# The reciprocal root of each norm in a two-layer decoder trunk: its six short steps on GpSimd's queue instead of VectorE's

## The chip, the core and the metric

The kernel runs on one core of one Trainium2 chip. The core has five engines with a queue of their own each: TensorE (PE in the profile, with PEld for its weight loads), VectorE (DVE), ScalarE (ACT), GpSimd (POOL) and SyncE (SP, which here only issues DMAs). Each engine takes its instructions strictly in the order in which they stand in its queue and waits for semaphores of the others. The metric is the time of one execution on the device in microseconds (us); the number given for a kernel is the median of several runs.

## What is computed

The reference is a decoder trunk of two layers over 256 tokens of width 1024, in float32. Cut to what matters here:

```python
def _rms(x):
    y = xf * lax.rsqrt(jnp.mean(xf * xf, axis=-1, keepdims=True) + EPS)

for l in range(DEPTH):                       # DEPTH = 2
    mod = (silu(c) @ w_ada[l] + b_ada[l]).reshape(B, N_SUB, 3, D_MODEL)
    norm_mod(h, j) = _rms(h) * g_norm[l, j] * (1.0 + scale_j) + shift_j
    x = x + 0.5 * gate(0) * _swiglu(norm_mod(x, 0), w_ffn_up[l, 0], w_ffn_down[l, 0])
    x = x + gate(1) * _mixer(norm_mod(x, 1), ...)
    x = x + 0.5 * gate(2) * _swiglu(norm_mod(x, 2), w_ffn_up[l, 1], w_ffn_down[l, 1])
```

So six norms stand between the sub-layers, and each needs one reciprocal root per token. The mixer has three token mixers (a gated linear recurrence and two kinds of causal attention) between one input and one output projection.

## The kernel before

The 256 tokens are two tiles of 128 partitions, called t = 0 and t = 1 here. A sub-layer ends for a tile with the last products of its down (or output) projection (`dn`, `wo`), after which the next sub-layer's norm of this tile can start; the other tile's products run on TensorE meanwhile.

Every weight arrives as a float32 block `raw` of 128x1024 over SyncE's queue. ScalarE casts it to a high part `H` (L246) and VectorE subtracts to get the low part `L` (L247); these two long instructions, 320 of each, fill most of both engines' queues. Each product is three matmuls (H by high part, L by high part, H by low part of the activations `hTh`, `hTl`). VectorE also makes the modulation (`raw` times `cb`, L292 and L317), where `cb` is silu(c).

One norm of a tile goes through these steps:

1. `residual` (L444, L445 on VectorE): x gets its update, in two halves.
2. `norm_sq` (L396 on ScalarE): the sum of squares of each half into `ss`; L399 adds the halves to `v`.
3. `rsqrt` (L359, then L363 and L364 twice): a first guess of 1/sqrt(v) from the bits of v, and two Newton steps. The result is `ny`. L399 and these five are the six short steps, each on 128x1 elements and each needing the one before.
4. `norm_xn` (L407 on ScalarE): `xn` = x times `ny`, two halves.
5. `norm_out`: TensorE transposes `xn` into `tp` (L418, eight 128x128 pieces in two buffers), ScalarE (L426) and VectorE (L428) make `hf` from it, and L431 to L434 split that into `hTh` and `hTl`, which the next projection (`pj` in the mixer, `up` in the feed-forward part) reads.

The buffers of `tp` are shared with the transposes `tg` (L532) and `tx` (L637) of other work: two in all.

The two norms of the input at the start have no L399 and take their sum of squares on VectorE (L936): 2 chains of five steps, and 10 chains of six later (there is no norm behind the last sub-layer).

The order of the instructions in each queue isn't the order of the code: the framework schedules the program with an estimate of each instruction's duration and writes each queue down in the order that it found. So a change of one engine's work can move rows on all.

Of the kernel before, what the change touches and what calls it, by code (L numbers as in the profile page):

```python
# [12 lines left out]
I32 = mybir.dt.int32  # L13
AF = mybir.ActivationFunctionType
ALU = mybir.AluOpType
# [79 lines left out]
def trunk_kernel(ctx: ExitStack, tc: tile.TileContext, x, c, wst, ada, par, cst, row, wg, out):  # L95
    nc = tc.nc
# [16 lines left out]
    def W2(shape, dt=F32, name="w2"):  # L113
        return w2.tile(shape, dt, tag="w2", name=name)

    def SM(shape, dt=F32, name="sm"):
        return sm.tile(shape, dt, tag="sm", name=name)
# [10 lines left out]
    V, A, T, S = nc.vector, nc.scalar, nc.tensor, nc.sync  # L128
# [224 lines left out]
            ada_step(1)  # L353


    def rsqrt(v, n, name):
        y = SM([128, n], name=name + "y")
        a = SM([128, n], name=name + "a")
        V.tensor_scalar(out=y.bitcast(I32), in0=v.bitcast(I32), scalar1=-0.5, scalar2=float(0x5F1FFFF9),  # L359
                        op0=ALU.mult, op1=ALU.add)  # L360
        for c in (-2.38924456, -3.0 / NEWTON ** 2):
            if n == 1:
                V.tensor_scalar(out=a, in0=y, scalar1=v, scalar2=y, op0=ALU.mult, op1=ALU.mult)  # L363
                V.tensor_scalar(out=y, in0=a, scalar1=c, scalar2=y, op0=ALU.add, op1=ALU.mult)  # L364
            else:
                V.tensor_tensor(out=a, in0=y, in1=y, op=ALU.mult)
                V.tensor_tensor(out=a, in0=a, in1=v, op=ALU.mult)
                V.scalar_tensor_tensor(out=y, in0=a, scalar=c, in1=y, op0=ALU.add, op1=ALU.mult)
        return y


# [12 lines left out]
    xn_t, r_t = {}, {}  # L384

    def norm_in(t):
        norm_sq(t, 2)
        norm_xn(t)

    def norm_sq(t, parts=1):  # L390
        n = D // parts
        ss = SM([128, parts], name="ss")
        for i in range(parts):
            q = slice(i * n, (i + 1) * n + i // (parts - 1) if parts > 1 else D + 1)
            junk = W2([128, D + 1], BF16, name="junk")
            A.activation(junk[:, q], xe[t][:, q], AF.Square, scale=1.0 / 32, accum_out=ss[:, i:i + 1])  # L396
        if parts == 2:
            v = SM([128, 1], name="v")
            V.tensor_tensor(out=v, in0=ss[:, 0:1], in1=ss[:, 1:2], op=ALU.add)  # L399
        else:  # L400
            v = ss
        r_t[t] = rsqrt(v, 1, "n")

    def norm_xn(t):
        xn_t[t] = W4([128, D], name="xn")
        for q in (slice(0, D // 2), slice(D // 2, D)):
            A.activation(xn_t[t][:, q], xt[t][:, q], AF.Copy, scale=r_t[t])  # L407
# [65 lines left out]
    def ffn(l, s, after, pre={}):  # L473
# [66 lines left out]
        def down(j, t):  # L540
            if j == 0:
                dn[t] = [PD([128, 512], name="dn") for _ in range(2)]
            w = [unit(("dn", l, s, j, i)) for i in range(2)]

            order = [(i, n) for i in range(2) for n in range(2)]
            for i, n in sorted(order, key=lambda p: p[1]) if j == NCH - 1 else order:
                q = slice(n * 512, (n + 1) * 512)
                mm3(dn[t][n], *gT[j, i, t], w[i][0][:, q], w[i][1][:, q],
                    j == 0 and i == 0, j == NCH - 1 and i == 1)
            if j == NCH - 1:  # L550
                if after is None:
                    residual(l, j3, t, dn[t], lambda t, q: S.dma_start(out=out[t * 128:(t + 1) * 128, q], in_=xt[t][:, q]))
                    return
                residual(l, j3, t, dn[t])
                norm_sq(t, 2)
                if t == 1:
                    norm_xn(1)
                    pending.append(lambda: after[1](1))
# [373 lines left out]
    for t in range(NT):  # L932
        ss = SM([128, 1], name="ss")
        junk = W2([128, D + 1], BF16, name="junk")
        x1 = xe[t][:, 0:D + 1]
        V.scalar_tensor_tensor(out=junk, in0=x1, scalar=1.0 / D, in1=x1, op0=ALU.mult, op1=ALU.mult, accum_out=ss)  # L936
        r_t[t] = rsqrt(ss, 1, "n")
        norm_xn(t)
    xnT = [W4([128, NT, 4, 128], name="xnT") for _ in range(2)]
    for g in range(2):  # L940
# [7 lines left out]
    for k in range(KT):  # L948
        for v in range(2):
# [3 lines left out]
                        scalar2=S_t[0, 0][:, k:k + 1], op0=ALU.mult, op1=ALU.add)  # L953
# [117 lines left out]
```

## Time and profile before

| | |
|---|---|
| median of 3 runs | 1011.37 us (1008.23 to 1013.19) |
| the profiled execution | 1010.85 us, of which the span from first to last instruction is 1009.0 us |
| TensorE busy | 982.2 us (97%) |
| VectorE busy | 761.4 us (75%), 1224 instructions |
| ScalarE busy | 532.9 us (53%) |
| GpSimd busy | 6.9 us, 16 instructions (12 are DMA issues) |

Rows of the trace give, for a timeline, the start in us, the length in us, the engine, the line of the kernel, the operation, what is written and read, and in brackets how long the engine sat idle before and what ended that. An arrow reads "written from", a number behind x counts merged instructions.

### The profile page before, as it was taken

Reading aid. Unit: us, or ns where it says so; the run is one execution under the profiler, and the core shown is the slowest. Engines: PE = TensorE matmul, PEld = TensorE weight load, DVE = VectorE, ACT = ScalarE, POOL = GpSimd, SP = SyncE. Lnnn points to the kernel's source line nnn. Section 1 sums busy time; section 2 is a strip of 40 time slices with the busy share of each in tenths; the row PEclk is TensorE's granted clock in tenths of the full one; section 3 lists DMA queues with packets and bytes.
Section 4 is the critical chain, followed back from the end, with each engine's and each line's share of the span. In section 5 each row is a group of like instructions: output and inputs, shape, how many; then the busy total and the mean of one; then the engine's idle time right before and its main releaser. Section 6 shows DMA issues by size and latency. Waiting matters only on the chain.

```text
span 1009.0 us, 15828 instructions
## 1 busy us (share of the span) xinstructions
PE 982.2 (97%) x6054; PEld 857.9 (85%) x6054; DVE 761.4 (75%) x1224; ACT 532.9 (53%) x854; POOL 6.9 (1%) x16
## 2 busy tenths in 40 slices
PE   6999999989999999999999999999999999999998
PEld 4999999867867799999878999997788778999996
DVE  8988888788996988888589888765778588636352
ACT  5373435558775534355465344455678655535340
POOL 0000000000000000000000000000000000000000
PEclk9999999999999999999999999999999999999999
DMA  8999999677382999999449999854542349655511
GB/s 320 352 336 341 350 330 342 237 259 268 127 279 96 318 370 331 343 327 329 171 165 339 361 346 335 310 177 157 189 167 84 105 155 343 241 180 192 185 64 42
DMA packets 69966, 251.26 MB, mean 249 GB/s; under 512 B 8066, under 2 KB 8706, under 8 KB 69891
## 3 DMA queue, kind: packets, MB, share of 16 engines
q1 hardware_dynamic: 68834, 247.09, 69.3%
q0 software_dynamic: 1056, 3.17, 1.0%
q8 instruction: 47, 0.77, 0.3%
q14 instruction: 29, 0.23, 0.1%
HBM read 249.16 MB, written 1.07 MB: 248 GB/s over the span
## 4 chain that ended last, share of the span: by engine, by line
PE 86%; DVE 7%; ACT 5%; issue 1%; DMA 1%; ACTq 0%; DVEq 0%; SPq 0%
PE up L470 38%; PE dn L258 8%; PE dn L260 8%; PE dn L259 8%; PE up L271 6%; PE pj L271 5%; PE up L273 3%; PE pj L273 2%; DVE L L247 2%; PE wo L258 1%; PE wo L259 1%; PE wo L260 1%; ACT hf L426 1%; ACT H L246 1%; DVE raw L292 1%
## 5 line engine op out<-in xcount | busy, mean ns | idle before, releaser
L247 DVE TENSOR_TENSOR L<-raw,H 128x1024 fp32r<-128x1024 f32 x320 | 381.5, 1220 | 79.1 <-ACT H L246 78.0
L246 ACT CAST H<-raw 128x1024 fp32r<-128x1024 f32 x320 | 327.9, 1051 | 114.1 <-DMA raw<-in_wst 61.3
L470 PE MATMUL up<-hTh,H 128*128 128x256 f32 x1088 | 209.9, 280 | 2.4 <-ACT H L246 1.9
L470 PE MATMUL up<-hTl,H 128*128 128x256 f32 x1088 | 210.0, 281 | 0.0
L470 PE MATMUL up<-hTh,L 128*128 128x256 f32 x1088 | 209.3, 280 | 0.0
L470 PEld LDWEIGHTS up<-hTh,H 128*128 128x128 f32 x1088 | 167.5, 188 | 8.8 <-ACT H L246 2.3
L470 PEld LDWEIGHTS up<-hTl,H 128*128 128x128 f32 x1088 | 163.8, 188 | 0.3 <-DVE hTl L955 0.3
L470 PEld LDWEIGHTS up<-hTh,L 128*128 128x128 f32 x1088 | 163.9, 189 | 0.0
L462 ACT ACTIVATE sg<-up 128x256 f32<-128x256 f32 x88 | 33.8, 384 | 209.5 <-PE up L470 168.1
L258 PE MATMUL dn<-H,gh 128*128 128x512 f32 x352 | 140.4, 399 | 1.3 <-ACT gh L535 1.1
L260 PE MATMUL dn<-H,gl 128*128 128x512 f32 x352 | 139.7, 397 | 0.0
L259 PE MATMUL dn<-L,gh 128*128 128x512 f32 x352 | 139.0, 395 | 0.0
L292 DVE SCALAR_TENSOR_TENSOR raw<-raw,cb 128x1024 f32<-128x1024 f32 x96 | 114.9, 1219 | 1.8 <-DMA raw<-in_ada 1.4
L260 PEld LDWEIGHTS dn<-H,gl 128*128 128x128 f32 x352 | 66.0, 188 | 16.0 <-DVE gl L536 0.9
L258 PEld LDWEIGHTS dn<-H,gh 128*128 128x128 f32 x352 | 66.2, 188 | 14.9 <-ACT gh L535 3.2
L519 DVE TENSOR_TENSOR sg<-sg,up 128x256 f32<-128x256 f32 x68 | 28.5, 419 | 65.6 <-ACT sg L462 65.1
L259 PEld LDWEIGHTS dn<-L,gh 128*128 128x128 f32 x352 | 66.2, 188 | 12.5
L271 PE MATMUL up<-H,hTh 128*128 128x512 f32 x160 | 64.8, 405 | 0.7 <-DVE hTh L431 0.6
L271 PE MATMUL up<-L,hTh 128*128 128x512 f32 x160 | 63.9, 400 | 0.0
L273 PE MATMUL up<-H,hTl 128*128 128x512 f32 x160 | 57.5, 396 | 0.0
L317 DVE SCALAR_TENSOR_TENSOR raw<-raw,cb 128x1024 f32<-128x1024 f32 x48 | 56.8, 1217 | 0.7 <-DMA raw<-in_ada 0.7
L271 PE MATMUL pj<-H,hTh 128*128 128x512 f32 x128 | 52.5, 410 | 1.2 <-DVE hTh L431 1.2
(229 smaller groups left out, 1051.5 us busy)
## 6 DMA issues: line engine op xcount, KB each, us to landing
raw<-in_wst SPq DMA_DIRECT2D x320, 512.0 KB, 5.2
raw<-in_ada SPq DMA_DIRECT2D x144, 512.0 KB, 5.3
gate<-row POOLq DMA_DIRECT2D x6, 512.0 KB, 6.9
x<-in_x SPq DMA_DIRECT2D x2, 512.0 KB, 4.3
wgt<-in_wg SPq DMA_DIRECT2D x2, 512.0 KB, 6.6
out_x<-x SPq DMA_DIRECT2D x4, 256.0 KB, 2.0
once<-in_cst SPq DMA_DIRECT2D x1, 192.0 KB, 5.4
p_sb<-in_par SPq DMA_DIRECT2D x1, 168.0 KB, 5.2
```

What stands on the lines that cost most here:

```text
L246: A.copy(h, raw)
L247: V.tensor_tensor(out=lo, in0=raw, in1=h.bitcast(F32), op=ALU.subtract)
L258: T.matmul(o, lhsT=xh, rhs=wh, start=first, stop=False)
L259: T.matmul(o, lhsT=xh, rhs=wl, start=False, stop=False)
L260: return T.matmul(o, lhsT=xl, rhs=wh, start=False, stop=last)
L271: T.matmul(o, lhsT=hh[:, k, :], rhs=part, start=k == 0 and i == 0, stop=False)
L273: mul = T.matmul(o, lhsT=hl[:, k, :], rhs=w(k)[0], start=False, stop=k == KT - 1)
L292: V.scalar_tensor_tensor(out=raw, in0=raw, scalar=1.0, in1=cb, op0=ALU.mult, op1=ALU.mult, accum_out=st[:, v, k:k + 1])
L317: V.scalar_tensor_tensor(out=raw, in0=raw, scalar=1.0, in1=cb, op0=ALU.mult, op1=ALU.mult, accum_out=col[:, k:k + 1])
L462: used.append(A.activation(*a, **k))
L470: return T.matmul(o[:, v], lhsT=w[:, q:q + 128], rhs=(hTh, hTl)[h][:, :, k, :], start=opens, stop=True, skip_group_check=True)
L519: V.tensor_tensor(out=sg, in0=sg, in1=o[:, 1], op=ALU.mult)
```

## The change

`rsqrt` and the addition of the two halves in `norm_sq` name GpSimd instead of VectorE. The arithmetic is the same. 70 short instructions (12 chains: 2 of five and 10 of six) leave VectorE's queue and come into GpSimd's.

```diff
-    def rsqrt(v, n, name):
-        y = SM([128, n], name=name + "y")
-        a = SM([128, n], name=name + "a")
-        V.tensor_scalar(out=y.bitcast(I32), in0=v.bitcast(I32), scalar1=-0.5, scalar2=float(0x5F1FFFF9),
+    def rsqrt(v, name):
+
+        G = nc.gpsimd
+        y = SM([128, 1], name=name + "y")
+        a = SM([128, 1], name=name + "a")
+        G.tensor_scalar(out=y.bitcast(I32), in0=v.bitcast(I32), scalar1=-0.5, scalar2=float(0x5F1FFFF9),
                         op0=ALU.mult, op1=ALU.add)
         for c in (-2.38924456, -3.0 / NEWTON ** 2):
-            if n == 1:
-                V.tensor_scalar(out=a, in0=y, scalar1=v, scalar2=y, op0=ALU.mult, op1=ALU.mult)
-                V.tensor_scalar(out=y, in0=a, scalar1=c, scalar2=y, op0=ALU.add, op1=ALU.mult)
...
+            G.tensor_scalar(out=a, in0=y, scalar1=v, scalar2=y, op0=ALU.mult, op1=ALU.mult)
+            G.tensor_scalar(out=y, in0=a, scalar1=c, scalar2=y, op0=ALU.add, op1=ALU.mult)
         return y
...
-            V.tensor_tensor(out=v, in0=ss[:, 0:1], in1=ss[:, 1:2], op=ALU.add)
+            nc.gpsimd.tensor_tensor(out=v, in0=ss[:, 0:1], in1=ss[:, 1:2], op=ALU.add)
```

Line numbers behind `rsqrt` are smaller by three in the changed kernel (L404 is what L407 was, L415 what L418 was). In GpSimd's queue each step waits on a semaphore for the one before; ahead of the first step stands one new instruction, a reload of the engine's library that waits for nothing. The DMA issues of `row` and `gate`, which were the queue's only work, keep their places between the chains, and none of them stands between the steps of a chain.

The schedule moves with it. The place shown first is the norm of tile 1 between the first layer's mixer and its second feed-forward part. VectorE's queue there, before:

```order
L445 TENSOR_TENSOR x_89<-x_89,tmp 128x512 x2
L247 TENSOR_TENSOR L<-raw,H 128x1024
L399 TENSOR_TENSOR v<-ss 128x1
L247 TENSOR_TENSOR L<-raw,H 128x1024
L359 TENSOR_SCALAR ny<-v 128x1
L495 TENSOR_TENSOR sg<-sg,up 128x256
L363 TENSOR_SCALAR na<-ny,v 128x1
L247 TENSOR_TENSOR L<-raw,H 128x1024
L364 TENSOR_SCALAR ny<-na,ny 128x1
L247 TENSOR_TENSOR L<-raw,H 128x1024
L363 TENSOR_SCALAR na<-ny,v 128x1
L247 TENSOR_TENSOR L<-raw,H 128x1024
```

And now:

```order
L442 TENSOR_TENSOR x_89<-x_89,tmp 128x512 x2
L247 TENSOR_TENSOR L<-raw,H 128x1024 x4
L492 TENSOR_TENSOR sg<-sg,up 128x256
L247 TENSOR_TENSOR L<-raw,H 128x1024
L425 TENSOR_SCALAR hf<-tp,G_2701,S_2702 128x128 x3
```

The short steps are gone from between the long ones, and four L247 follow each other. ScalarE's queue at the same place, before:

```order
L396 ACTIVATE junk,ss<-x_89 128x513
L246 CAST H<-raw 128x1024
L462 ACTIVATE sg<-up 128x256
L246 CAST H<-raw 128x1024
L407 ACTIVATE xn<-x_89,ny 128x512 x2
L462 ACTIVATE sg<-up 128x256
L426 ACTIVATE hf<-tp,S_2702,G_2701 128x128 x4
```

And now:

```order
L393 ACTIVATE junk,ss<-x_89 128x513
L246 CAST H<-raw 128x1024
L404 ACTIVATE xn<-x_89,ny 128x512 x2
L459 ACTIVATE sg<-up 128x256
L246 CAST H<-raw 128x1024
L423 ACTIVATE hf<-tp,S_2702,G_2701 128x128 x4
```

`xn` now stands ahead of an `sg` and a cast that stood ahead of it. TensorE's queue at the same place, with the tiles' numbers, from the last matmuls of the row `up` of tile 0 on, before:

```order
L273 MATMUL up_3522<-H_3585,hTl_138 128x512
L418 MATMUL tp_3556<-c_sb_94,xn_3467 128x128 x4
L418 MATMUL tp_3568<-c_sb_94,xn_3467 128x128 x4
L532 MATMUL tg_3598<-c_sb_94,sg_3519 128x128 x2
L258 MATMUL dn_3640<-H_3644,gh_3601 128x512
L271 MATMUL up_3605<-H_3473,hTh_137 128x512
```

And now:

```order
L415 MATMUL tp_3556<-c_sb_94,xn_3467 128x128 x4
L415 MATMUL tp_3568<-c_sb_94,xn_3467 128x128 x4
L271 MATMUL up_3522<-H_3549,hTh_137 128x512
L271 MATMUL up_3522<-L_3550,hTh_137 128x512
L273 MATMUL up_3522<-H_3549,hTl_138 128x512
L271 MATMUL up_3522<-H_3585,hTh_137 128x512
L271 MATMUL up_3522<-L_3586,hTh_137 128x512
L273 MATMUL up_3522<-H_3585,hTl_138 128x512
L271 MATMUL up_3522<-H_3585,hTh_137 128x512
L271 MATMUL up_3522<-L_3586,hTh_137 128x512
L273 MATMUL up_3522<-H_3585,hTl_138 128x512
L529 MATMUL tg_3598<-c_sb_94,sg_3519 128x128 x2
```

The eight transposes stand nine matmuls earlier: behind 39 of the 48 matmuls of this row of `up`, not behind all. The other norms of tile 1 move alike: behind 39 instead of 48 in both mixers' input and in the second layer's second feed-forward part (in the second layer's mixer input it was 44), behind 33 instead of 47 in front of the second layer. For tile 0 the transposes move by seven matmuls behind the first feed-forward part of layer 0, and by none or one elsewhere.

The second place is the start of ScalarE's queue, before:

```order
L407 ACT_TABLE_LOAD
L407 ACTIVATE xn<-x_88,ny 128x512
L152 ACTIVATE le<-le 128x8
L154 ACT_TABLE_LOAD
L182 ACTIVATE cb<-pc 128x512 x2
L407 ACTIVATE xn<-x_88,ny 128x512
L407 ACTIVATE xn<-x_89,ny 128x512 x2
```

And now:

```order
L152 ACT_TABLE_LOAD
L152 ACTIVATE le<-le 128x8
L154 ACT_TABLE_LOAD
L182 ACTIVATE cb<-pc 128x512
L404 ACTIVATE xn<-x_88,ny 128x512
L182 ACTIVATE cb<-pc 128x512
L404 ACTIVATE xn<-x_88,ny 128x512
L404 ACTIVATE xn<-x_89,ny 128x512 x2
```

The first half of `xn` stood ahead of everything; now it stands between the two halves of `cb`.

## Rows read from the trace of the kernel before

**Rows 1.** The page: busy times by engine, and one of its costliest groups.

```profile
PE 982.2 (97%) x6054; PEld 857.9 (85%) x6054; DVE 761.4 (75%) x1224; ACT 532.9 (53%) x854; POOL 6.9 (1%) x16
...
L246 ACT CAST H<-raw 128x1024 fp32r<-128x1024 f32 x320 | 327.9, 1051 | 114.1 <-DMA raw<-in_wst 61.3
```

**Rows 2.** Stretches around the norms: busy time by engine, granted clock, DMA share, GB/s.

```profile
190.00:230.00 40.00, 35.91 (x157) 27.54 (x156) 31.93 (x64) 23.39 (x40) 1.09 (x2) 0.96 0.64 221
300.00:345.00 45.00, 43.12 (x195) 33.92 (x193) 36.33 (x71) 26.85 (x49) 0.00 (x0) 1.00 0.55 186
345.00:495.00 150.00, 150.00 (x1028) 138.53 (x1027) 120.62 (x168) 67.48 (x91) 1.09 (x2) 1.00 0.93 331
495.00:540.00 45.00, 43.90 (x201) 34.99 (x200) 35.55 (x67) 24.45 (x44) 0.00 (x0) 1.00 0.47 158
690.00:725.00 35.00, 33.52 (x154) 26.44 (x154) 26.60 (x48) 24.69 (x41) 0.00 (x0) 1.00 0.46 150
790.00:835.00 45.00, 43.12 (x194) 33.76 (x189) 32.11 (x62) 24.18 (x45) 0.00 (x0) 0.96 0.44 147
```

**Rows 3.** Waits: engine, line, releaser: us in total, times, longest.

```profile
ACT xn L407 <- DVE ny L364: 25.7, 8, 5.9
PE tg L532 <- ACT hf L426: 3.1, 3, 1.0
PE tx L637 <- ACT lxt L634: 2.4, 2, 1.7
```

**Rows 4.** Timeline, VectorE: first and last steps of tile 1's norm behind layer 0's mixer.

```profile
326.92 0.16 DVE L399 TENSOR_TENSOR v<-ss 128x1 f32<-128x1 f32 x1
327.00 1.22 DVE L247 TENSOR_TENSOR L<-raw,H 128x1024 fp32r<-128x1024 f32 x1
...
332.42 0.21 DVE L364 TENSOR_SCALAR ny<-na,ny 128x1 f32<-128x1 f32 x1
```

**Rows 5.** Timelines of ScalarE and TensorE at the same place.

```profile
326.69 0.20 ACT L396 ACTIVATION_READ_ACCUMULATOR junk<-x 128x1 f32 x1
...
332.66 1.34 ACT L407 ACTIVATE xn<-x,ny 128x512 f32<-128x512 f32 x2 [3.56 <-DVE ny L364]
334.19 1.50 ACT L426 ACTIVATE hf<-tp,S,G 128x128 f32<-128x128 f32 x4
...
321.87 0.50 PE L271 MATMUL up<-H,hTh 128*128 128x512 f32 x1 [0.28 <-DVE hTh L431]
...
333.44 1.27 PE L418 MATMUL tp<-c_sb,xn 128*128 128x128 f32 x8
335.75 0.44 PE L532 MATMUL tg<-c_sb,sg 128*128 128x128 f32 x2 [1.04 <-ACT hf L426]
336.65 0.50 PE L258 MATMUL dn<-H,gh 128*128 128x512 f32 x1 [0.46 <-ACT gh L535]
```

**Rows 6.** Timeline, VectorE: first and last of six steps with nothing between them.

```profile
504.61 0.15 DVE L399 TENSOR_TENSOR v<-ss 128x1 f32<-128x1 f32 x1
...
505.86 0.21 DVE L364 TENSOR_SCALAR ny<-na,ny 128x1 f32<-128x1 f32 x1
```

**Rows 7.** Timeline, GpSimd: one of its four memsets and one of its DMA issues.

```profile
0.28 0.10 POOL L1060 MEMSET const-float32-1.0<- 128x1 f32 x1
...
549.02 0.54 POOL L324 DMA_DIRECT2D row<-gt  x1 [184.12 <-DVE gt L322]
```

**Rows 8.** Stretches of 4 us behind two of TensorE's pauses, columns as in rows 2.

```profile
224.00:228.00 4.00, 4.00 (x15) 3.24 (x14) 2.00 (x5) 1.64 (x2) 0.54 (x1) 0.68 0.51 169
828.00:832.00 4.00, 4.00 (x14) 3.15 (x13) 4.00 (x8) 1.38 (x2) 0.00 (x0) 0.66 0.63 209
```

**Rows 9.** Timeline of the start.

```profile
5.67 0.15 DVE L359 TENSOR_SCALAR ny<-ss 128x1 int32<-128x1 int32 x1
...
9.10 1.09 ACT L182 ACTIVATE cb<-pc 128x512 f32<-128x512 f32 x2
...
10.62 1.22 DVE L292 SCALAR_TENSOR_TENSOR raw<-raw,cb 128x1024 f32<-128x1024 f32 x1
```

More of the change, by code (lines that the diff above doesn't have):

```diff
@@ L353, in ada_until @@
             ada_step(1)
-    def rsqrt(v, n, name):
-        y = SM([128, n], name=name + "y")
-        a = SM([128, n], name=name + "a")
-        V.tensor_scalar(out=y.bitcast(I32), in0=v.bitcast(I32), scalar1=-0.5, scalar2=float(0x5F1FFFF9),
+    def rsqrt(v, name):
[3 more added lines that the diff above has]
+        G.tensor_scalar(out=y.bitcast(I32), in0=v.bitcast(I32), scalar1=-0.5, scalar2=float(0x5F1FFFF9),
                         op0=ALU.mult, op1=ALU.add)
         for c in (-2.38924456, -3.0 / NEWTON ** 2):
-            if n == 1:
-                V.tensor_scalar(out=a, in0=y, scalar1=v, scalar2=y, op0=ALU.mult, op1=ALU.mult)
-                V.tensor_scalar(out=y, in0=a, scalar1=c, scalar2=y, op0=ALU.add, op1=ALU.mult)
[L365 to L368, printed above, removed]
+            G.tensor_scalar(out=a, in0=y, scalar1=v, scalar2=y, op0=ALU.mult, op1=ALU.mult)
+            G.tensor_scalar(out=y, in0=a, scalar1=c, scalar2=y, op0=ALU.add, op1=ALU.mult)
         return y
@@ L398, in norm_sq @@
             v = SM([128, 1], name="v")
-            V.tensor_tensor(out=v, in0=ss[:, 0:1], in1=ss[:, 1:2], op=ALU.add)
+            nc.gpsimd.tensor_tensor(out=v, in0=ss[:, 0:1], in1=ss[:, 1:2], op=ALU.add)
         else:
             v = ss
-        r_t[t] = rsqrt(v, 1, "n")
+        r_t[t] = rsqrt(v, "n")
     def norm_xn(t):
@@ L936, in trunk_kernel @@
         V.scalar_tensor_tensor(out=junk, in0=x1, scalar=1.0 / D, in1=x1, op0=ALU.mult, op1=ALU.mult, accum_out=ss)
-        r_t[t] = rsqrt(ss, 1, "n")
+        r_t[t] = rsqrt(ss, "n")
         norm_xn(t)
```

## The prediction

> **What bounds the kernel now.** I read the page's busy times first: TensorE is busy 97% of the span, VectorE 75% and GpSimd 1% [rows 1]. So what a change can win is TensorE's idle time, and I looked for it by stretches. Between the norms there is none: 345 to 495 us is 150.00 busy of 150 [rows 2]. Around the norms there is: 4.09, 1.88, 1.10, 1.48 and 1.88 us in the five stretches, together 10.4 us [rows 2]. The waits say who holds things up: ScalarE's `xn` waits 25.7 us in 8 waits for the last short step on VectorE, and TensorE's `tg` waits for `hf`, three steps behind `xn` [rows 3].
>
> The timeline shows why the root is late. Behind layer 0's mixer the sum of squares of tile 1 is ready at 326.89 (326.69 + 0.20) [rows 5]; the last step ends at 332.63 (332.42 + 0.21) [rows 4]. The chain takes C = 5.7 us, because each step waits behind a long instruction such as the 1.22 us of L247 [rows 4]. With nothing between them six steps take 1.46 us (504.61 to 506.07) [rows 6]. TensorE meanwhile comes to `tg` and waits 1.04 us for the buffer that `hf` must free, then 0.46 us for `gh` [rows 5].
>
> **The change, part by part.** It removes the steps from VectorE. I count nothing for VectorE's own time: it isn't the bound, and its work behind 326 us is casts for weights that TensorE needs later.
>
> It puts the steps on GpSimd. No row shows such a step there. The nearest from below is GpSimd's memset, 0.10 us, which makes 0.6 us for six; the nearest from above is its DMA issue, 0.54 us, 3.2 us for six [rows 7]. VectorE's own six give 0.24 each (1.46 / 6) [rows 6]. A dependent step with scalars from memory is nearer to the issue than to a memset, and I take 0.45, so 2.7 us. To this I add 0.9 us for meeting VectorE (three quarters of one 1.22 us instruction [rows 4]), which gives C = 3.6 us. The bound from above is a step that each time waits out a long instruction: 6 x 1.22 + 2.7 = 10 us.
>
> What C may be is set by TensorE's new order. At the place of rows 5 the row of `up` starts at 321.87 and its 48 matmuls end with the transposes' start at 333.44, 0.241 us each. Behind 39 of them the transposes are due at 331.27. A half of `xn` takes some 0.67 us (1.34 for two), so the root must be there by 330.6, C at most 3.7. `hf` must be done when TensorE comes to `tg`, at 334.7 as before (333.44 + 1.27; the same work in another order). In the old order `hf` ends 3.03 us after `xn` starts (332.66 to 334.19 + 1.50), with an `sg` between; the new order adds a cast of 1.05 us [rows 1], so 4.1 us, which again asks for 330.6 [rows 5]. So with C = 3.6 the two waits of 1.5 us go, and with C = 5.4 they are back in another place.
>
> The five stretches one by one at C = 3.6. Of the 10.4 us of idle time some stays: `tx` follows `pj` directly in the new order too and waits for a copy of its last result, some 0.7 us in each layer (2.4 us in two waits, the longest 1.7 [rows 3]), and 0.28 us before `up` of tile 0 behind each mixer, where the transposes don't move [rows 5]. That leaves 10.4 - 1.4 - 0.6 = 8.4 us. At the layer boundary the transposes move by 14 matmuls, not 9, so that C may be only some 3.0 us there: 0.6 back. Small overshoots at the other places: 0.4.
>
> Behind two of the pauses the granted clock falls between its two levels, to 0.68 and 0.66 over 4 us [rows 8], which is (0.32 + 0.34) x 4 = 2.6 us of TensorE's time. At a pause of about the same size, behind layer 0's mixer, the stretch 300 to 345 shows 1.00 [rows 2]. I count half, 1.3 us.
>
> The start: `xn` of tile 0 now stands between the halves of `cb`, and VectorE's first long instruction on `cb` starts at 10.62 [rows 9]. The sum of squares is there at 5.67; with C = 2.7 + 0.9, less one step, a half of `xn` and half of the 1.09 us of `cb`, it would be 5.67 + 3.2 + 0.7 + 0.5 = 10.1. I book 0.5 us of loss for the library's reload ahead of it, whose length no row shows. More is hidden by nothing: every us over 10.62 delays the modulation that TensorE's first projection waits for.
>
> The Trainium skill (GPSIMD Engine Reference, Instruction dispatch) gives about 6 us for the first call to freshly loaded code on this engine, with no instruction visible. If that runs from the program's start, it would end at about 7 us and cost an estimated 1.5 us more, so the sum would be 1.5 us smaller by it; no row here shows it.
>
> Sum: 8.4 + 1.3 - 0.6 - 0.4 - 0.5 = 8.2 us. The profiled execution took 1010.85 us, so 1002.6; the median of the runs is 0.5 above it, and I forecast **1003 us**.
>
> Beyond 3.6 us every us of C costs on seven chains (five of tile 1, two of tile 0 behind feed-forward parts), about 7 us per us of C, as TensorE stands in order behind its earlier transposes. The gain is used up at C = 3.6 + 8.2 / 7 = 4.8 us.
>
> **The rivals.**
>
> *The two engines hold each other up.* Before, VectorE's queue was what paced the steps. If a step of GpSimd can't start while a long VectorE instruction with two inputs in SBUF runs, the pace stays: the queue shows four L247 in a row at this place, and VectorE is busy nearly throughout. v waits from 326.9 to 328.2, then 0.45, then 1.22, and so on until the fourth L247 is done; then VectorE waits for `sg`, which now stands behind `xn`, and the last two steps run free. 1.3 + 3 x 1.2 + 3 x 0.45 ends near 333, C about 5.5 to 6 here, 2.7 behind the mixers for tile 0, where VectorE has nothing to do, and about 5 on the mean. Against the forecast that is 7 x 1.4 = 9.8 us: 1013 us, in a range from 1009 to 1017. For it: VectorE's 36.33 of 45 us [rows 2]. Against: nothing in the trace shows GpSimd beside VectorE at all; its issue of 0.54 us was no longer than the others.
>
> The Trainium skill (SBUF — State Buffer, Who interferes with whom) states this rule: an instruction of VectorE with two SBUF inputs contends with one of GpSimd that reads SBUF, and whichever starts first keeps the shared port pair to its end. By it the time would be that of this rival. No run shown so far bears it out or against it.
>
> *The steps themselves are slow.* At 1 us each, with nothing in their way, C is 6 everywhere: 8.2 - 2.4 x 7 = -8.6, so 1020 us, slower. It decides from 0.8 us for a step on. For it: apart from memsets the only job of this engine in the trace takes 0.54 us [rows 7]. Against: its memset took 0.10.
>
> *The reload is long.* If the engine is ready at 15 us, the start comes 8 us later and eats the gain: 1011 us.
>
> *The gain is taken elsewhere.* The earlier `xn` pushes casts of weights and `sg` back on ScalarE, and TensorE waits for those: 1007 us. Against it: DMA and ScalarE have room (a DMA share of 0.44 to 0.64 and 23.39 of 40 to 26.85 of 45 us [rows 2]).
>
> **How the numbers follow.** The forecast 0.42; the engines holding each other up 0.25; gain taken elsewhere 0.16; slow steps 0.10; reload 0.07. The range for 8 in 10 goes from 998 (everything won, with the full clock part) to 1016. The forecast's own range is 999 to 1006. A measurement of this kernel tells 0.5%, 5 us, from no change (its own runs lie 5 us apart). Faster by over 0.5%: the forecast's 0.42 and 0.05 of the others, 0.47. Slower: slow steps 0.10 and 0.09 of the lock and the reload, 0.19. Within: 0.34.
>
> **What would show it.** GpSimd's six steps with a start-to-start near 0.45 us, and chains of 3 to 4 us from the end of `junk` to `xn`. `xn`'s waits down from 25.7 us to some 10. TensorE's idle time in the five stretches down from 10.4 to about 3, `tg`'s wait for `hf` gone, and the granted clock 1.00 behind 224 us and 828 us. The forecast is wrong if steps start only where VectorE's long instructions end, if a step takes 0.8 us or more alone, or if VectorE's first instruction on `cb` starts later than 11 us.

## The result

The changed kernel takes 1019.61 us (median of 6 runs, 1015.95 to 1022.91) against 1011.42 us: a ratio of 1.0082, with a 95% interval from 1.0065 to 1.0099. The change made the kernel slower by 0.8%, where 1003 us had been forecast. The profiled run took 1017.62 us, its span 1015.8 us.

The busy times by stretch, as in [rows 2], a little longer where the work now ends later:

```profile
190.00:232.00 42.00, 37.11 (x160) 28.24 (x159) 30.82 (x49) 24.61 (x41) 12.33 (x14) 0.96 0.56 196
300.00:347.00 47.00, 44.73 (x204) 35.00 (x204) 33.72 (x62) 25.78 (x47) 6.36 (x12) 1.00 0.48 160
...
495.00:542.00 47.00, 44.70 (x198) 35.81 (x197) 31.42 (x53) 22.84 (x42) 6.77 (x12) 0.96 0.45 151
690.00:728.00 38.00, 34.69 (x158) 26.89 (x157) 22.87 (x36) 22.58 (x39) 8.53 (x12) 1.00 0.37 129
790.00:841.00 51.00, 48.93 (x223) 36.75 (x222) 30.75 (x49) 27.86 (x51) 6.36 (x12) 0.97 0.34 109
```

TensorE's idle time (length less its busy time) is 4.89, 2.27, 2.30, 3.31 and 2.07 us in these. The first stretch ends too early: the wait at `tx`, which lay at 223 us before, comes later now.

```profile
239.09 0.66 PE L634 MATMUL tx<-c_sb,lxt 128*128 128x128 f32 x4 [1.16 <-ACT lxt L631]
```

With these 1.16 us the sum is 16.0 us instead of 10.4; it had been forecast to fall to about 3. The fifth busy time is GpSimd's, 12.33 us in 14 instructions in the first stretch. The waits for the root (engine, line, releaser: us in total, times, longest), against [rows 3], and those of TensorE for `xn`, before (L418) and now (L415):

```profile
ACT xn L404 <- POOL ny L365: 34.4, 10, 7.0
...
PE tp L418 <- ACT xn L407: 1.5, 2, 1.0
...
PE tp L415 <- ACT xn L404: 11.4, 6, 3.2
```

ScalarE's wait is longer than the 25.7 us of before, and TensorE now waits for `xn` for 11.4 us, where it was 1.5. GpSimd's timeline shows why: steps of the start, a chain beside an idle VectorE, and the chain at the place of [rows 4].

```profile
5.69 0.18 POOL L361 TENSOR_SCALAR ny<-ss 128x1 int32<-128x1 int32 x1 [5.24 <-DVE ng L150]
...
314.90 0.19 POOL L396 TENSOR_TENSOR v<-ss 128x1 f32<-128x1 f32 x1 [83.73 <-ACT junk L393]
...
315.48 0.34 POOL L364 TENSOR_SCALAR na<-ny,v 128x1 f32<-128x1 f32 x1
...
316.73 0.26 POOL L365 TENSOR_SCALAR ny<-na,ny 128x1 f32<-128x1 f32 x1
...
328.30 3.36 POOL L396 TENSOR_TENSOR v<-ss 128x1 f32<-128x1 f32 x1 [11.30 <-ACT junk L393]
331.75 0.19 POOL L361 TENSOR_SCALAR ny<-v 128x1 int32<-128x1 int32 x1
...
333.29 0.26 POOL L365 TENSOR_SCALAR ny<-na,ny 128x1 f32<-128x1 f32 x1
```

VectorE at the same place, and its first instruction on `cb` at the start (10.62 us before [rows 9]):

```profile
10.25 1.22 DVE L292 SCALAR_TENSOR_TENSOR raw<-raw,cb 128x1024 f32<-128x1024 f32 x1
...
326.98 4.63 DVE L247 TENSOR_TENSOR L<-raw,H 128x1024 fp32r<-128x1024 f32 x4
```

The add `v`, 0.19 us long at 314.90, lasts 3.36 us at 328.30. It ends at 331.66, just when VectorE's run of four L247 ends (326.98 + 4.63 = 331.61). The other five steps then take as long as at 315 us. ScalarE's sum of squares and `xn`, and TensorE's waits for these:

```profile
328.02 0.20 ACT L393 ACTIVATION_READ_ACCUMULATOR junk<-x 128x1 f32 x1
...
333.59 1.33 ACT L404 ACTIVATE xn<-x,ny 128x512 f32<-128x512 f32 x2 [4.43 <-POOL ny L365]
```

```profile
220.24 1.44 PE L415 MATMUL tp<-c_sb,xn 128*128 128x128 f32 x8 [3.22 <-ACT xn L404]
334.36 1.27 PE L415 MATMUL tp<-c_sb,xn 128*128 128x128 f32 x8 [1.80 <-ACT xn L404]
524.81 1.84 PE L415 MATMUL tp<-c_sb,xn 128*128 128x128 f32 x8 [2.30 <-ACT xn L404]
720.39 1.27 PE L415 MATMUL tp<-c_sb,xn 128*128 128x128 f32 x8 [1.65 <-ACT xn L404]
830.78 1.27 PE L415 MATMUL tp<-c_sb,xn 128*128 128x128 f32 x8 [1.79 <-ACT xn L404]
```

From 328.22 (328.02 + 0.20) to 333.55 the chain takes C = 5.33 us. Read in the same way, the seven chains of the forecast (five of tile 1, two of tile 0 behind the first feed-forward parts) took 5.46 us on the mean before (38.2 / 7) and take 5.44 now (38.1 / 7). On the mean the root comes no earlier. But TensorE's transposes were moved forward as if it did, and stand waiting at all five places of tile 1. The span of the profiled execution grew by 6.8 us (1009.0 to 1015.8): 5.6 us are the added idle time of the five stretches, 2.1 us are added busy time of TensorE (982.2 to 984.3), and some 0.8 us come back at the start.

### The profile page after: what moved, and what is told of

It reads as the page before. It is cut to its first block, busy times and chain, and to the rows that moved or that the text cites. A ratio compares the mean times of both kernels' runs of the same rounds, so it can differ in the third digit from the quotient of the medians.

```text
span 1015.8 us, 15836 instructions
## 1 busy us (share of the span) xinstructions
PE 984.3 (97%) x6054; PEld 859.5 (85%) x6054; DVE 751.4 (74%) x1154; ACT 531.2 (52%) x854; POOL 50.1 (5%) x86
## 3 DMA queue, kind: packets, MB, share of 16 engines
HBM read 249.16 MB, written 1.07 MB: 246 GB/s over the span
## 4 chain that ended last, share of the span: by engine, by line
PE 84%; ACT 5%; POOL 4%; DVE 3%; issue 2%; DMA 1%; SPq 0%; ACTq 0%; DVEq 0%
PE up L467 38%; PE dn L260 8%; PE dn L259 8%; PE dn L258 7%; PE up L271 5%; PE pj L271 4%; PE up L273 3%; PE pj L273 2%; ACT H L246 1%; PE wo L258 1%; PE wo L259 1%; PE wo L260 1%; POOL v L396 1%; POOL na L364 1%; DMA raw<-in_wst 1%
## 5 line engine op out<-in xcount | busy, mean ns | idle before, releaser
L247 DVE TENSOR_TENSOR L<-raw,H 128x1024 fp32r<-128x1024 f32 x320 | 381.7, 1221 | 75.5 <-ACT H L246 74.0
```

What stands on the lines that cost most here:

```text
L247: V.tensor_tensor(out=lo, in0=raw, in1=h.bitcast(F32), op=ALU.subtract)
```

## The experiments

The theory (A): GpSimd's steps are held while VectorE works through its casts, and the loss comes because the order was written for an early root. Its rivals are that GpSimd's steps or handovers are late by themselves (B), and that the early order loses by itself (C). The table has all timed kernels; C is the mean over the seven chains, "early" means transposes of tile 1 behind 33 to 39 of their row's 48 matmuls, "late" behind 44 to 48.

| kernel | steps | order | C, us | median, us | ratio to before |
|---|---|---|---|---|---|
| before | VectorE, between casts | late | 5.46 | 1011 to 1012 | 1 |
| v_early | VectorE, between casts | early | 5.46 | 1015.68 | 1.0038 (1.0021 to 1.0055) |
| t0_only | GpSimd for tile 0 | late | 5.52 | 1014.0 | 1.0020 (1.0007 to 1.0034) |
| changed | GpSimd | early | 5.44 | 1019.61 | 1.0082 (1.0065 to 1.0099) |
| pool_memset | GpSimd | early | 4.83 | 1014.65 | 1.0033 (1.0018 to 1.0048) |
| late_tp | GpSimd | late | 5.60 | 1028.26 | 1.0154 (1.0134 to 1.0173) |
| pool_free | GpSimd, VectorE still | early | 2.43 | 1008.29 | 0.9957 (0.9941 to 0.9973) |
| pool_one_cast | the same, one cast ahead | early | 2.41 | 1002.07 | 0.9906 (0.9891 to 0.9922) |
| v_first | VectorE, next to each other | early | 1.79 | 1006.65 | 0.9937 (0.9923 to 0.9951) |
| v_one_cast | the same, one cast ahead | early | 2.37 | 999.49 | 0.9888 (0.9869 to 0.9906) |

**The hold taken away: VectorE stands still (pool_free).** A copy on VectorE waits for the root, and the casts of tile 1's row are queued behind it:

```diff
         r_t[t] = rsqrt(v, "n")
+        seen = SM([128, 1], name="seen")
+        root_last[:] = [V.tensor_copy(seen, r_t[t])]
...
             if (j, t) == (1, 0):
                 hold.append(1)
+                root_end[:] = root_last
...
+        with tc.issue_after(root_end[-1].ins) if root_end else nullcontext():
+            V.tensor_tensor(out=lo, in0=raw, in1=h.bitcast(F32), op=ALU.subtract)
```

> The changed kernel, steps on GpSimd, with one short copy of the root on VectorE that waits for the last step; the casts of weights of the row that runs meanwhile are queued behind that copy, so VectorE stands still while GpSimd does the chain. The transposes stand as in the changed kernel. Theory A (the hold by VectorE's instructions is the cause): steps take 0.2 to 0.35 us each, the chain about 2.1 us and the handover to VectorE some 0.2 us, so 1002 to 1008 us, 12 to 17 us below the changed kernel. Rival B (GpSimd's steps or the handover between engines are late by themselves): 1014 us or more, while the kernel with the steps next to each other on VectorE is fast. Rival C (the early order loses by itself): both are at 1012 us or more.

1008.29 us, 11 us below the changed kernel with the same engines and the same early transposes. B falls, and so does C as it was put here, for an early order with an early root; what that order costs with a late one is measured further below (v_early). The copy is made behind each of the ten later chains: C of tile 0's two falls as well, from 5.38 and 4.67 us to 3.46 and 2.61. The time is just above what was expected, since TensorE now waited for a cast, up to 2.48 us at a place.

**The same on VectorE (v_first).** The kernel before, with the casts queued behind the chain's last step in the same way:

```diff
-                V.tensor_scalar(out=y, in0=a, scalar1=c, scalar2=y, op0=ALU.add, op1=ALU.mult)
+                root_last[:] = [V.tensor_scalar(out=y, in0=a, scalar1=c, scalar2=y, op0=ALU.add, op1=ALU.mult)]
```

> The kernel before, all steps on VectorE, but the casts of weights of the row that runs meanwhile (L247) are queued behind the last step of tile 1's chain, so that the six steps stand next to each other on VectorE. The transposes then stand as early as in the changed kernel (behind 33 to 39 of 48 matmuls). Theory A: the root comes 1.5 to 2.5 us behind the sum of squares, the transposes wait little, and the gain that was forecast for C at most 3.6 us comes: 1002 to 1007 us. Rival C (the early order loses by itself, through casts and rows of sg pushed back on ScalarE and the clock behind the pauses): 1012 us or more.

1006.65 us. GpSimd isn't needed for the gain: steps next to each other are.

**One cast let ahead of the chain (pool_one_cast, v_one_cast).** The hold begins at the row's second weight block:

```diff
+                if (j, t) == (1, 0) and k > 1:
+                    root_end[:] = root_last
```

> The kernel with VectorE standing still for GpSimd's chain, but the first cast of the row (L247) is let ahead. Theory A: the cast is over about when the sum of squares is there, the steps are held little, the waits of 2.48, 2.47, 1.57, 1.48 and 1.47 us for casts shrink to 1 us or less: 1001 to 1005 us, still 1 to 3 us above its VectorE twin since the chain takes 2.1 us instead of 1.5 and ends with a handover. Rival: the cast holds the first step by over 1 us, and the time stays at 1007 to 1010 us.

> The kernel with the steps next to each other on VectorE, but the first cast of the row (L247) is let ahead of tile 1's chain; the others stay behind it. There TensorE waited 1.95, 1.94, 1.17, 0.70 and 0.58 us for such a cast, and VectorE stood idle for 1.2 us ahead of the chain. Theory A: these waits go and the chain starts no later, so 4 to 8 us less than 1006.7: 999 to 1003 us. Rival: the cast pushes the chain back and the transposes wait for it instead, 1005 to 1008 us.

1002.07 and 999.49 us: both as theory A expected, and both below the kernel before, by 0.9 and 1.1%. The timelines of pool_one_cast behind layer 0's mixer, VectorE, GpSimd and TensorE:

```profile
321.31 1.22 DVE L248 TENSOR_TENSOR L<-raw,H 128x1024 fp32r<-128x1024 f32 x1
324.74 0.15 DVE L404 COPY seen<-ny 128x1 f32<-128x1 f32 x1 [2.22 <-POOL ny L368]
...
322.62 0.19 POOL L399 TENSOR_TENSOR v<-ss 128x1 f32<-128x1 f32 x1 [10.05 <-ACT junk L396]
...
326.08 0.50 PE L272 MATMUL up<-L,hTh 128*128 128x512 f32 x1 [1.07 <-DVE L L248]
```

The cast ends at 322.53, the add starts at 322.62 and no step is longer than 0.34 us. `xn` follows at 324.74, and no transposes wait for it. Behind VectorE's 2.22 us of standing still TensorE waits 1.07 us for a cast; in the twin on VectorE it waits 0.55 us there:

```profile
324.92 0.50 PE L272 MATMUL up<-L,hTh 128*128 128x512 f32 x1 [0.55 <-DVE L L248]
```

**The early order alone (v_early).** The kernel before, with the rest of the row queued behind the transposes:

```diff
                 if mid and mid[0] == k:
                     mid[1](mul)
+                    if norm_tp:
+                        early.enter_context(tc.issue_after(norm_tp[-1].ins))
```

> The kernel before, all steps on VectorE between its casts as before, but the rest of TensorE's row is queued behind tile 1's transposes, so that these stand behind 31 to 39 of the 48 matmuls, as in the changed kernel. Theory A: the root comes 5 to 6 us behind the sum of squares as before, and TensorE waits for it 1.6 to 3.2 us at five places, as in the changed kernel: 1014 to 1021 us with no step on GpSimd at all. Rival: the loss of the changed kernel is GpSimd's own (handover, tile 0's chains), and the early order costs nothing on VectorE: 1008 to 1013 us.

1015.68 us, a loss of 0.38% with no step on GpSimd. TensorE waits for `xn` at the same five places as in the changed kernel, at the fourth 0.50 us against 1.65 (the profiled execution, 1017.58 us, was the longest of ten):

```profile
221.82 1.27 PE L421 MATMUL tp<-c_sb,xn 128*128 128x128 f32 x8 [1.57 <-ACT xn L410]
...
336.30 1.76 PE L421 MATMUL tp<-c_sb,xn 128*128 128x128 f32 x8 [2.21 <-ACT xn L410]
...
528.04 1.97 PE L421 MATMUL tp<-c_sb,xn 128*128 128x128 f32 x8 [2.70 <-ACT xn L410]
...
832.07 1.27 PE L421 MATMUL tp<-c_sb,xn 128*128 128x128 f32 x8 [2.19 <-ACT xn L410]
```

**Tile 0's chains alone (t0_only).** Tile 1's go back to VectorE:

```diff
-        r_t[t] = rsqrt(v, "n")
+        r_t[t] = rsqrt(v, "n", V if t else nc.gpsimd)
```

> The changed kernel with the chains of tile 1 back on VectorE; those of tile 0 and of the start of tile 0 stay on GpSimd. Theory A: the loss sits in the five late chains of tile 1 (transposes moved by 9 to 14 matmuls), so 1008 to 1012 us, the kernel before or up to 2 us less, from the 0.4 us at the start and tile 0's chains behind the mixers, which run beside an idle VectorE. Rival: the chains of tile 0 behind the feed-forward parts lose as well (their steps took 0.6 to 1.3 us each beside VectorE), then 1013 to 1016 us.

1014.0 us, a loss of 0.20%, in the rival's range. The profiled execution, at 1017.0 us the longest of twelve, shows two waits of TensorE behind layer 1's first feed-forward part (0.51 and 0.21 us of waits there before, and 0.76 us at `tx`):

```profile
707.55 0.50 PE L258 MATMUL dn<-H,gh 128*128 128x512 f32 x1 [1.64 <-ACT gh L530]
...
724.60 0.51 PE L271 MATMUL pj<-H,hTh 128*128 128x512 f32 x1 [1.48 <-DVE hTh L426]
```

The first of these waits, 1.64 us, is in the changed kernel too (at 706.15); the second isn't, and C of tile 0's two chains is no longer than before on the sum (5.39 and 4.68 us against 6.27 and 4.23). So what the rival says is likely for the first wait and not shown for the whole 0.20%. Of the changed kernel's 0.8%, then, the early order by itself can make some 0.4 and tile 0's chains at most some 0.2; that the two add up isn't shown, and some 0.2 stay over in any case. C at the first mixer's input, 6.98 us now against 5.82, may be part of that.

**Late transposes with GpSimd's chain (late_tp).** The table that says behind which of a row's eight steps the transposes may come:

```diff
-K_T = (4, 2, 4)
+K_T = (7, 7, 7)
```

> The changed kernel, but the transposes of tile 1 may stand no earlier than behind the last multiple of the row (47 of its 48 matmuls or all of them), as they did before the change; the steps stay on GpSimd. Theory A (GpSimd's steps are held while VectorE works through a run of long instructions, and the loss arises because TensorE's transposes were moved ahead of the point at which the root is there): the root comes as late as in the changed kernel (about 5.3 us behind the sum of squares at the second norm of layer 0's mixer output), but the transposes wait for nothing, so 1009 to 1013 us, 7 to 10 us below the changed kernel. Theory B (a late root costs the same wherever the transposes stand): no change, 1017 to 1021 us.

1028.26 us: a miss for both theories. The edit moves more than the transposes. TensorE's timeline behind layer 0's mixer, and ScalarE's:

```profile
340.10 0.44 PE L529 MATMUL tg<-c_sb,sg 128*128 128x128 f32 x2 [2.23 <-ACT hf L423]
342.43 0.77 PE L271 MATMUL up<-H,hTh 128*128 128x512 f32 x1 [1.88 <-DVE hTh L428]
...
335.83 1.34 ACT L404 ACTIVATE xn<-x,ny 128x512 f32<-128x512 f32 x2 [4.44 <-POOL ny L365]
...
338.55 1.50 ACT L423 ACTIVATE hf<-tp,S,G 128x128 f32<-128x128 f32 x4
```

`hf` starts 2.72 us behind `xn` (1.53 in [rows 5]) because two `sg` and a cast stand between, and `up` of tile 1 follows `tg` at once, where `dn` stood before. The transposes came late, but what follows them was ordered anew too. This run doesn't isolate the transposes and is no evidence for A. It also shows that the place of the transposes isn't the only part of the order that counts: it has them where they stood before and nearly the C of before (5.60 us), and takes 16 us more.

**What holds a step (three benches).** The first puts the steps beside different VectorE instructions:

```python
    for n, op, pool_work in ((0, None, chain), (1, two, chain), (2, two, chain), (4, two, chain), (8, two, chain),
                             (4, one, chain), (8, half_psum, chain), (4, accum, chain), ...
```

> A bench that leaves the whole decoder out (it only copies x to the output) and puts GpSimd's six steps beside runs of VectorE instructions that start some 0.4 us earlier: none; 1, 2, 4 and 8 of the cast's subtraction with two inputs in SBUF (1.2 us each); 4 one-input instructions; 8 with one input in PSUM; 4 of the modulation's kind with an accumulator; 4 with a wait for ScalarE between each two; and a long GpSimd instruction (one input, 128x1024) beside 4 of either kind. Theory A1 (a step of GpSimd is held until VectorE's run of such instructions ends, however long): the first step lasts about 0.9, 2.1, 4.4 and 9 us beside 1, 2, 4 and 8, the other five 0.2 to 0.35 us each; beside PSUM inputs all six take 0.2 to 0.35 us; with waits between VectorE's instructions the first step ends in the first pause, after about 1 us. Rival A2 (held only to the end of the instruction that runs): the first step lasts about 0.9 us beside any number, and each of the next steps up to 1.2 us. Rival B (GpSimd's steps are of uneven length by themselves): long steps beside nothing or beside PSUM inputs too.

Four subtractions, then one-input instructions, then inputs from PSUM, on VectorE and GpSimd:

```profile
22.89 5.02 DVE L151 TENSOR_TENSOR L<-raw,H 128x1024 fp32r<-128x1024 f32 x4
...
40.70 2.90 DVE L155 TENSOR_SCALAR J<-raw 128x1024 f32<-128x1024 f32 x4
...
23.18 0.97 POOL L172 TENSOR_TENSOR v<-ss 128x1 f32<-128x1 f32 x1 [0.96 <-ACT ss L170]
24.25 1.16 POOL L175 TENSOR_SCALAR ny<-v 128x1 int32<-128x1 int32 x1
...
40.92 0.51 POOL L172 TENSOR_TENSOR v<-ss 128x1 f32<-128x1 f32 x1 [3.64 <-ACT ss L170]
...
45.49 0.19 POOL L172 TENSOR_TENSOR v<-ss 128x1 f32<-128x1 f32 x1 [0.96 <-ACT ss L170]
```

Beside inputs from PSUM nothing is held, and without a VectorE run the six steps take 0.19 to 0.34 us, so rival B is out. Beside the others each step waits for the next boundary (the end of one VectorE instruction and the start of the next). That is rival A2, not A1. With a pause of 0.26 us behind each VectorE instruction the add takes 1.10 us. The hold goes the other way as well: beside one GpSimd instruction of 128x1024 (3.72 us) the four subtractions take 5.79 us instead of 5.02, and beside another (3.60 us) the four one-input instructions 4.37 instead of 2.90. But these subtractions all write one tile and each waits for the one ahead. The second bench gives them tiles of their own:

```diff
-        V.tensor_tensor(out=L[0], in0=raw, in1=H.bitcast(F32), op=ALU.subtract)
+        V.tensor_tensor(out=L[i], in0=raw, in1=H.bitcast(F32), op=ALU.subtract)
```

> A second bench without the decoder (it only copies x to the output). In the first bench all of VectorE's subtractions wrote the same tile, so each waited for the one ahead on its own engine, and GpSimd got one step in at each boundary (0.97, 1.17, 1.32, 1.10 us); in the changed kernel, where four subtractions write tiles of their own and wait for nothing at hand, one step lasted 3.36 us through three of them. Here: 4 subtractions that write one tile, then 1, 2, 4 and 8 that write tiles of their own, then 8 of these with a memset of 128x1 between each two, then 4 one-input instructions that write tiles of their own. Theory A1' (the hold passes only where VectorE's next instruction has to wait or doesn't read two SBUF operands): the first step lasts about 0.9, 2.1, 4.4 and 9 us beside 1, 2, 4 and 8, and about 1 us where memsets stand between, one step for each subtraction there. Rival A2 (it passes at each instruction, and the 3.36 us have another reason): about 1 us in all of them.

Beside eight of these, which start at 33.40 and last 1.14 us each:

```profile
33.62 1.04 POOL L169 TENSOR_TENSOR v<-ss 128x1 f32<-128x1 f32 x1 [0.96 <-ACT ss L167]
34.75 1.04 POOL L172 TENSOR_SCALAR ny<-v 128x1 int32<-128x1 int32 x1
35.90 3.31 POOL L175 TENSOR_SCALAR na<-ny,v 128x1 f32<-128x1 f32 x1
```

Neither theory fits: two steps pass at the next boundary, the third only after three. Memsets between changed nothing here (1.04, 1.05, 3.34 us). The third bench sorts by the kind of step, here those with both scalars from memory:

```python
            G.tensor_scalar(out=n, in0=z, scalar1=ss[:, 1:2], scalar2=ss[:, 1:2], op0=ALU.mult, op1=ALU.mult)
```

> A third bench without the decoder (it only copies x to the output). In the second bench the add v and the first guess ny got in at the next boundary between two of VectorE's subtractions (1.04 us each) and the step na, whose two scalars are loaded from memory, only after two or three (2.25 and 3.31 us); in the changed kernel the add lasted 3.36 us at three places. Here 8 subtractions that write tiles of their own: with one pair of inputs for all and the six steps; with inputs of their own (as in the kernel) and the six steps; then with inputs of their own and six equal steps of one kind: six adds, six with fixed scalars, six with scalars from memory. Theory K (the kind of GpSimd's step decides): adds and fixed scalars last 1 us each, those with scalars from memory 2 to 3.4 us. Rival M (VectorE's side decides, by whether its next inputs lie ready): with inputs of their own the add is held for 2 to 3 subtractions too, and the kinds don't differ.

Six two-input steps (called adds; the bench multiplies), six with fixed scalars, six with both scalars from memory, beside eight subtractions (of the first two kinds the last five steps are shown):

```profile
44.78 5.60 POOL L168 TENSOR_TENSOR ta<-ta,ss 128x1 f32<-128x1 f32 x5
...
54.91 5.59 POOL L176 TENSOR_SCALAR tf<-tf 128x1 f32<-128x1 f32 x5
64.00 3.22 POOL L184 TENSOR_SCALAR tl<-ss 128x1 f32<-128x1 f32 x1 [3.50 <-ACT ss L200]
```

Theory K holds in the bench: two-input steps and fixed scalars take 1.12 us each (5.60 / 5), one boundary; the first step with both scalars from memory takes 3.22 us, three. The root's `na` is of that kind (3.31 us here too), and its `ny`, with one scalar from memory, took 2.17. It doesn't carry over whole: in the changed kernel it is the add that took 3.36 us.

**Memsets between the casts in the changed kernel (pool_memset).** Behind each cast of tile 1's row:

```diff
+        if part:
+            with tc.issue_after(sub.ins):
+                V.memset(nil, 0.0)
```

> The changed kernel with a memset of 128x1 on VectorE behind each cast (L247) of the row in which tile 1's chain runs. Theory A1': the first step ends at the first memset, within about 1.2 us, instead of after 3.36, but the next steps then meet the next casts; the chain takes 4 to 5.3 us instead of 5.3, so 1012 to 1020 us: one step for each cast costs nearly as much as one wait for all. Rival A2: the memset changes nothing, steps of 3.4 us stay. If the hold alone were the price and each handover were free, 1002 to 1008 us.

1014.65 us, 5 us less than the changed kernel and inside the range of A1'. Behind layer 0's mixer the add now passes at a boundary. VectorE and GpSimd:

```profile
328.24 2.37 DVE L248 TENSOR_TENSOR L<-raw,H 128x1024 fp32r<-128x1024 f32 x2
...
330.53 1.22 DVE L248 TENSOR_TENSOR L<-raw,H 128x1024 fp32r<-128x1024 f32 x1
...
329.56 1.10 POOL L400 TENSOR_TENSOR v<-ss 128x1 f32<-128x1 f32 x1 [11.30 <-ACT junk L397]
330.75 1.05 POOL L365 TENSOR_SCALAR ny<-v 128x1 int32<-128x1 int32 x1
```

The chain takes 3.94 us instead of 5.33, and two other places of the seven show the same. But the schedule moved too: three casts stand beside the chain, not four, and VectorE's run ends 2.19 us behind the start of the add (331.75 - 329.56) instead of 3.31 us (331.61 - 328.30). In both kernels the held steps end with the run. So 1.1 of the 1.4 us come from the shorter run, and what the memsets do by themselves isn't shown. The mean C falls by 0.61 us for 5 us of time.

## Why the prediction was wrong

*The price of a step: a little too high.* 0.45 us was taken; alone, six steps take 2.09 us (314.90 to 316.99), 0.35 each, against 2.7 us in the sum. The rival of slow steps is out.

*Meeting VectorE: the step that failed.* The sum added 0.9 us, three quarters of one cast, as if only one step met a cast. Measured is 5.44 - 2.09 = 3.35 us on the mean of the seven chains. That is the rival in which the two engines hold each other up, with its place and nearly its size: it had a mean C of about 5. It assumed one step for each cast; in the kernel one add waited through three casts at three places, and `na` through two at others, with the same end. Its price, 7 x 1.4 us, gave 1013; with the measured C it is 7 x 1.84 = 12.9 us over the forecast, 1016, and 4 us to the result stay unexplained by it. The 1020 us of the rival of slow steps lie nearer to the result, by chance: it asked for 1 us a step with nothing in its way. The Trainium skill (SBUF — State Buffer, Who interferes with whom) states that VectorE instructions with two SBUF inputs and GpSimd instructions that read SBUF exclude each other, and that one with a single SBUF input outside the two-port modes doesn't contend. The traces agree: steps of 0.19 us beside PSUM inputs, 0.97 us and more beside two SBUF inputs. They differ from its wording that the loser is blocked for the whole instruction of the other: a step was held through up to three. Beside VectorE's one-input instructions in SBUF steps were held too (0.51 us for an add); which mode those ran in, no run shows.

*What an early root is worth: the total right, its terms not.* With C = 2.41 us on GpSimd's own steps the kernel takes 1002.07 us, 1 us from the forecast, and on VectorE 999.49. But part of that agreement is luck. The busy times of the five stretches together with 345 to 495 us, where TensorE is never idle, for pool_one_cast and v_one_cast, and the page of pool_one_cast:

```profile
sum 360.00, PE 352.69 PEld 299.24 DVE 279.57 ACT 195.19 POOL 17.97; mean PE 58.78 PEld 49.87 DVE 46.60 ACT 32.53 POOL 3.00
...
sum 360.00, PE 356.29 PEld 302.90 DVE 295.61 ACT 195.27 POOL 1.63; mean PE 59.38 PEld 50.48 DVE 49.27 ACT 32.55 POOL 0.27
...
PE 977.3 (98%) x6054; PEld 856.1 (86%) x6054; DVE 751.6 (75%) x1164; ACT 531.2 (53%) x854; POOL 29.1 (3%) x86
```

In pool_one_cast the idle time falls from 10.4 to 7.3 us, by 3.1 where the sum had 7.4 (8.4 - 0.6 - 0.4); TensorE's busy time falls by 4.9 us (982.2 to 977.3), where the sum had 1.3 for the clock. One miss makes up for the other. In v_one_cast, where VectorE doesn't stand still for another engine, the idle time is 3.7 us, 6.7 less, close to what was added up.

The slope of about 7 us for 1 us of C fits two pairs: 17.5 us for 3.03 us between the changed kernel and pool_one_cast (5.8), 5 us for 0.61 with the memsets (8.1). C alone doesn't set the time, though: pool_free has the C of pool_one_cast and takes 6 us more, v_early has the C of before and takes 4 us more.

*The break-even, C = 4.8 us: somewhat too high.* C is 0.6 above it and the kernel is slower. But pool_memset has just this C, 4.83, and is slower than before by 0.33%, and with C as before the early order alone costs 0.38%.

*The clock: too small in a good case, and no gain in this one.* 1.3 us were booked. Before, stretches of 4 us show 0.89 and 0.68 at 220 to 228 and 0.91 and 0.66 at 824 to 832, 3.4 us in all, and 0.79 and 0.78 at 16 to 24 us, 1.7 us more. In pool_one_cast and v_one_cast no stretch is below 0.99 but the one in which the span ends; the dip at 16 to 24 us lies ahead of these norms and is missing from the changed kernel too, so it can't be put down to them. In the changed kernel the stretches at 220 and 832 us show 0.65 and 0.57, and a new place appeared, 0.62 at 524 to 528, at the transposes' 2.30 us wait: a share between the levels of 2.4 and 1.2 GHz, behind a pause that was not there before. The sign of 1.00 behind 224 and 828 us didn't come.

*The start: wrong sign.* 0.5 us of loss were booked for the library's reload; VectorE's first instruction on `cb` comes 0.37 us earlier. GpSimd's first step is at 5.69, released by VectorE, so the reload ended before it was missed. The 6 us that the Trainium skill (GPSIMD Engine Reference, Instruction dispatch) gives for the first call are not to be seen ahead of any step that anything waited for.

*Of the signs named beforehand*, the steps' price where nothing holds them, the vanished wait of `tg` and the start came as forecast; the chains of 3 to 4 us, the shorter waits of `xn` and the idle time of 3 us did not, and "steps start only where VectorE's long instructions end" is what the timeline shows, as their ends.

Three things stay open: why the add is held through three casts in the kernel (3.36 us at 328, 518 and 824) and passes at the first boundary in the benches (0.97 to 1.04), with inputs of their own too; why the add passes at the first boundary in pool_memset (1.10 us), though memsets change nothing in the bench; and which cause makes the 2 of the 8 us that are left beside the early order and tile 0's chains.

## What to carry to other kernels

Moving short dependent steps to an idle engine didn't shorten their chain, because that engine was held while its neighbour worked: six steps of 2.1 us became 5.4 us on the mean beside VectorE's casts with two SBUF inputs, as long as before. What was wanted was an undisturbed chain, and queueing the neighbour's long instructions behind it, all but one, gave that without a change of engine (0.9888 of the time). And where a scheduler writes the queues down from assumed durations, an order written for an early result can cost time of its own when the result is late: with the same C of 5.46 us, the early transposes alone cost 0.38%.

## What the runs showed of the hardware

In the benches a GpSimd step of 0.19 to 0.34 us beside VectorE's subtractions of two SBUF tiles, where none of these waits for another, takes one boundary with two tile inputs or with fixed scalars (0.97 to 1.12 us), two with one scalar from memory (2.17) and three with both (3.22 to 3.31), as long as the run lasts. In the changed kernel an add took three (3.36 us). If each subtraction waits for the one ahead on its own engine, every kind passes at the next boundary (0.97 to 1.32 us), and the subtractions themselves are spaced 1.26 instead of 1.14 us. One-input VectorE instructions of 128x1024 hold it too (0.51 us for an add at 0.72 us each); instructions with one input from PSUM don't (0.19 us for an add).
